# A gated-attention encoder layer on one core: first gates asked for together, the sixth product of the output moved, x on another queue, and a planner that costs accumulated weights differently

## The chip, the core and the metric

The kernel runs on one core of a Trainium2 chip. Time is device time in microseconds. The core has five engines that run side by side, each in the order of its own instructions: TensorE (PE; its weight loads are listed as PEld), VectorE (DVE), ScalarE (ACT), GpSimd (POOL) and SyncE (SP). SP, ACT and POOL also issue DMA transfers, which 16 DMA engines carry out. Matmul results land in PSUM banks.

## What is computed

One layer of a streaming encoder with 512 tokens of width 2048. The input is normalized and multiplied by one wide matrix. Its columns serve three token mixers of four heads each (q, k, v and a gate path per head), a forget gate, and three merge gates of width 2048. The mixers are A (softmax attention with a cumulative forget bias), B (chunked attention with a relative bias) and C (stick-breaking attention). Cut to what matters:

```python
hn = rmsnorm(x, norm_g)
proj = jnp.einsum('bsd,dc->bsc', hn, w_in)
gates = jax.nn.sigmoid(proj[..., QKVG_COLS + N_HEADS:] + b_gate).reshape(b, s, N_BRANCH, D_MODEL)
...
ys = jnp.stack([from_heads(ya), from_heads(yb), from_heads(yc)], axis=2)
ys = ys * jax.nn.silu(br[:, :, :, 3])
up = jnp.einsum('bsnw,nwd->bsnd', ys, w_up)
merged = jnp.sum(gates * up, axis=2)
return x + jnp.einsum('bsd,de->bse', merged, w_out)
```

## The kernel before

**Products in three parts.** All operands are float32. A weight tile arrives in a buffer named raw (there are eight), ACT rounds it to wh (line 366), and DVE subtracts to get the rest, wl (line 371). The activations are split in the same way into a high and a low part. A product is then three matmuls: high by wh, low by wh, high by wl. There are three wh buffers and two wl buffers, so ACT and DVE work two or three units ahead of PE.

**Units.** The work of PE is a list of units, each with one weight tile of 128 × 2 × 512 numbers (512 KB). Line 265 issues their matmuls into banks named acc. The list begins with the first head of C and one gate group as plain products (two blocks of x, kt, to a unit; the first two units hold one each). Then come eleven groups of one head and one gate group, then the up-projections, and then the output in two halves (`out_task(0)` and `out_task(1)`).

**Seven products in place of eight.** A head and a gate group, or half of the output, form a 2 × 2 block product that is made by Strassen's scheme in Winograd's form: seven products, numbered here, in the plain order 5, 1, 6, 7, 4, 2, 3, each of four units of 12 matmuls. Products 5 and 7 need a difference or sum of two weight blocks: SP fetches the one, and POOL adds the other into the same buffer with an accumulating DMA (`add_up`, line 281). Products 6 and 3 load nothing. Their weights are made by DVE, which adds the raw of product 1 to that of product 5 for the sixth (`sum_up`, line 574), and later that of product 2 for the third. So the raw buffers of product 5 are held until product 3 has been split.

**The output's first half.** Its operands are the merged blocks m, of which the last four pairs are ready only when the last up-projection is done; they are turned by PE (line 1285) and combined and split by `merged_a` and `merged_b`. Its unit order is written by hand: products 5, 1 and 6 on the first two quarters of the depth, then the same on the other two, then 7, 4, 2, 3. Product 6 has its banks in att (the attention's pool) there, because 5 and 1 hold the four banks of acc. The second half uses the plain order.

**The merge gates.** Each gate block goes through HBM (`gl`). `gates_of` fetches one (tile sg) and takes its sigmoid on ACT (line 1235). `up_units` makes, for each of the column groups g = 0, 2, 1, 3 and each mixer b, two units over four banks (tb = 0 to 3); when a bank is done, DVE multiplies it by its gate (line 1251) and so frees it. The fetches are attached to positions in the unit list, before the units that use them: at the third last unit for tb 0 and 1, at the second last for tb 2 and 3.

**The planner.** The order of the instructions on PE, ACT and DVE is written out by a planner in the kernel (`Flow`). Each piece of work is a generator that yields what it waits for, or an engine, a cost and perhaps a due time. The planner keeps a clock per engine and always takes the piece that can start first, and of those the one with the earliest due time. When a transfer lands is believed from a model: `landing` for plain ones and `add_up` for accumulating ones, both on one shared `line`. SP and POOL aren't among the three engines; the framework orders their transfers itself.

**The start.** A burst of 42 products of a small identity matrix (`WARM`, line 417) precedes the first real product. The constants come on ACT's queue, x and the weights on SP's. For the first two blocks of x, ACT makes the high part straight from x, with the norm's weight as scale, and DVE the low part (lines 434 and 437); for the later ones x is scaled first (line 445 or 448) and then split (lines 246 and 250).

Of the kernel before, what the change touches and what calls it, by code (L numbers as in the profile page):

```python
# [8 lines left out]
F32 = mybir.dt.float32  # L9
F32R = mybir.dt.float32r  # L10
BF16 = mybir.dt.bfloat16
AF = mybir.ActivationFunctionType
# [3 lines left out]
P = 128  # L16
S = 512
# [9 lines left out]
CH = 4  # L27
# [1 line left out]
HS = S // 2  # L29
EPS = 1e-6  # L30
NEG = -1e30
WARM = 42
SCALE = HD ** -0.5
LA = 2

A, B, C = 0, 1, 2
Q, K, V, G = 0, 1, 2, 3
PE, ACT, DVE = 0, 1, 2
# [116 lines left out]
def act_us(n, x=1):  # L155
    return x * (0.075 + 0.00095 * n)


def dve_us(n, x=1):
    return x * (0.1 + 0.00105 * n)  # L160
# [3 lines left out]
def hybrid_kernel(  # L164
# [12 lines left out]
    nc = tc.nc  # L177
    PS = bass.MemoryType.PSUM

    cp = ctx.enter_context(tc.tile_pool(name="cp", bufs=1))  # L180
    xp = ctx.enter_context(tc.tile_pool(name="xp", bufs=NX))
    wp = ctx.enter_context(tc.tile_pool(name="wp", bufs=3))
    tp = ctx.enter_context(tc.tile_pool(name="tp", bufs=NT))
# [7 lines left out]
    def nm(s):  # L191
        uid[0] += 1
        return f"{s}_{uid[0]}"

    flow = Flow()
# [4 lines left out]
    def t2(s, dt=F32):  # L200
        return tp.tile([P, S], dt, tag="t2", name=nm(s))
# [7 lines left out]
    def att():  # L209
        return pt.tile([P, S], F32, tag="att", name=nm("att"))  # L210

    def f(ap):
        return ap.bitcast(F32)
# [6 lines left out]
    def two(ap):  # L220

        return ap.rearrange("p (h s) -> p h s", h=2)
# [20 lines left out]
    def split(hi, lo, src, n, ev=None, due=(), hi_ev=None):  # L243

        yield (ACT, act_us(n), *due)
        nc.scalar.activation(hi, src, AF.Copy)  # L246
        if hi_ev is not None:
            set_(hi_ev)
        yield (DVE, dve_us(n), *due)
        nc.vector.tensor_sub(lo, src, f(hi))  # L250
        if ev is not None:
            set_(ev)
# [15 lines left out]
    line = [0.0, 0.0]  # L268
# [7 lines left out]
    def fetch(to, src, ready, kb):  # L276
        nc.sync.dma_start(to, src)
        return Event(landing(ready, kb))

    def add_up(to, src, ready, kb):  # L280
        nc.gpsimd.dma_start(to, src, accum_op=ALU.add)  # L281
        line[1] = max(line[1], ready + 1.0) + kb / 170.0
        return Event(line[1] + 2.5)

    def stored(slots, n, kb):

        slots.free += [landing(flow.fin, kb)] * n
# [1 line left out]

    nc.scalar.preload_act_table_set("natural_log_exp_and_others")  # L290
    small_in = cp.tile([P, consts.shape[1]], F32, name="small_in")
    nc.scalar.dma_start(small_in, consts)
    gn = small_in[:, 0:KT]
    gqk = small_in[:, KT:KT + 4]
    bfc = small_in[:, KT + 4:KT + 5]
    wf = small_in[:, KT + 5:].rearrange("p (k h) -> p k h", h=NH)

    epsc = cp.tile([P, 1], F32, name="epsc")
    nc.gpsimd.memset(epsc, EPS)
    nhepsc = cp.tile([P, 1], F32, name="nhepsc")  # L300
# [8 lines left out]
    identb = cp.tile([P, P], BF16, name="identb")  # L309
# [26 lines left out]
    units = []  # L336
    side = {}

    def at(u, g, slack=5.0):
        side.setdefault(u, []).append((g, slack))  # L340
# [20 lines left out]
    def prep(u):  # L361
        n = u.shape[0] * S
        u.hi = wp.tile([P] + u.shape, F32R, tag="wh", name=nm("wh"), bufs=LA + 1)
        yield u.there
        yield ACT, act_us(n)
        nc.scalar.activation(u.hi, u.raw, AF.Copy)  # L366
        set_(u.ready_hi)
        yield wls, 1
        u.lo = wp.tile([P] + u.shape, F32R, tag="wl", name=nm("wl"), bufs=LA)
        yield DVE, dve_us(n)  # L370
        nc.vector.tensor_sub(u.lo, u.raw, f(u.hi))  # L371
        set_(u.ready)
        u.split_done()
# [38 lines left out]
    xraw, x_in = [None] * KT, [Event() for _ in range(KT)]  # L412
    first_ps = att()
    atts.free.pop()
    nc.vector.memset(first_ps, 0.0)
    for _ in range(WARM):
        nc.tensor.matmul(first_ps[:, :P], identb, identb, start=True, stop=True)
    xps.free.clear()


# [5 lines left out]
    def prep_x(kt):  # L426

        due = (5.0 + 3.2 * kt,)
        yield x_in[kt]
        x = xraw[kt]  # L430
        if kt < 2:
            g = gn[:, kt:kt + 1]
            yield (ACT, act_us(S), *due)
            nc.scalar.activation(xs[kt].hi, two(x), AF.Copy, scale=g)
            set_(raw_hi[kt])
            yield (DVE, dve_us(S), *due)
            nc.vector.scalar_tensor_tensor(xs[kt].lo, two(x), g, f(xs[kt].hi), op0=ALU.mult, op1=ALU.subtract)
            set_(raw_ev[kt])
            yield (DVE, 0.5, due[0] + 5.0)
            nc.vector.tensor_scalar_mul(x, x, g)  # L440
            set_(scaled[kt])
            return
        if kt < 10:
            yield (DVE, 0.5, *due)
            nc.vector.tensor_scalar_mul(x, x, gn[:, kt:kt + 1])
        else:
            yield (ACT, 0.65, *due)
            nc.scalar.activation(x, x, AF.Copy, scale=gn[:, kt:kt + 1])
        set_(scaled[kt])
        yield from split(xs[kt].hi, xs[kt].lo, two(x), S, raw_ev[kt], due, raw_hi[kt])  # L450
# [127 lines left out]
    PLAIN = [(p, c) for p in (5, 1, 6, 7, 4, 2, 3) for c in range(CH)]  # L578
# [649 lines left out]
    def gates_of(n, g, tb):  # L1228
        yield last_head.event("hl", 2)
        yield t2s, 1  # L1230
        t = sig[n, g, tb] = t2("sg")
        yield fetch(t, gl[n, g, tb], flow.now, 256)
        yield last_head.event("g")
        yield ACT, act_us(S) + 0.1
        nc.scalar.activation(t, t, AF.Sigmoid)  # L1235
        set_(sig_ev[n, g, tb])
# [41 lines left out]
    def turned_m(g, i):  # L1278
        for tb in range(QB):
            yield merged_ev[NB - 1, g, tb]  # L1280
        yield atts, 1
        yield PE, 0.11 * QB
        ps = att()
        for tb in range(QB):
            nc.tensor.transpose(ps[:, blk(tb)], merged[g, tb][:, blk(i)], identf)  # L1285
        turns[g] = turns.get(g, 0) + 1
        if turns[g] == QB:
            give(t2s, QB)
        yield t2s, 1
        yield ACT, act_us(S)  # L1290
        m = t2("m")
        nc.scalar.activation(m, ps, AF.Copy)
        give(atts)
        k = 4 * g + i
        if k < UK:
            kept_m[k] = m
            spawn(merged_a(k, m), 4.0, flow.fin)
        else:
            spawn(merged_b(k - UK, m), 3.0, flow.fin)
# [48 lines left out]
    for g in (0, 2, 1, 3):  # L1348
        for b in range(NB):
            for tb in range(QB):  # L1350
                at(len(units) - 3 + tb // 2, lambda n=(C, B, A)[b], g=g, tb=tb: gates_of(n, g, tb))
            units.extend(up_units(g, b))
        for i in range(QB):
            at(len(units) - 1, lambda g=g, i=i: turned_m(g, i))
# [6 lines left out]
    def out_task(i):  # L1361
        where = dict(c11=(0, 0), c12=(2, 0), c21=(0, 1), c22=(2, 1))

        def place(name, tb):
            b, q = where[name]
            return b + tb, 2 * i + q

        def done(name, tb, c):
            yield ACT, 0.05
            nc.scalar.dma_start(out[place(name, tb)[0], place(name, tb)[1]], c)  # L1370
            stored(t2s, 1, 256)

        def rest(name, tb):
            return xn[place(name, tb)[0], place(name, tb)[1]]

        def src(m, half, c):
            return w_out[2 * i + m, CH * half + c]

        order, other = PLAIN, ()
        if i == 0:  # L1380
            order = [(p, c) for cs in ((0, 1), (2, 3)) for p in (5, 1, 6) for c in cs]
            order += PLAIN[3 * CH:]
            other = (6,)
        return Strassen(src, mops, done, order, other, rest).units

    for i in range(2):
        units.extend(out_task(i))


    def loads():  # L1390
        def x(kt):
            yield t2s, 1
            xraw[kt] = t2("x")
            x_in[kt].t = fetch(xraw[kt], xT[kt], 0.0, 256).t

        def n(i):
            n_in[i].t = fetch(xnat[i // 2][:, i % 2, :], xn[i // NQ, i % NQ], 0.0, 256).t

        order = [("x", 0), ("w", 0), ("x", 1), ("w", 1), ("x", 2), ("x", 3), ("w", 2)] + [("n", i) for i in range(4)]
        order += [("x", 4), ("x", 5), ("w", 3)] + [("n", i) for i in range(4, 8)]  # L1400
        order += [("x", 6), ("x", 7), ("w", 4)] + [("n", i) for i in range(8, 12)]
        order += [("x", 8), ("x", 9), ("w", 5)] + [("n", i) for i in range(12, 16)]
        for i in range(6, 9):
            order += [("x", 2 * i - 2), ("x", 2 * i - 1), ("w", i)]
        for kind, i in order:
            if kind == "x":
                yield from x(i)
            elif kind == "n":
                n(i)
            else:  # L1410
                yield from units[i].load()
        for u in units[9:]:
            yield from u.load()
# [12 lines left out]
                spawn(u.after(), 0.0, flow.fin)  # L1426

    line[0] = 0.8
    flow.fin = 5.0
    spawn(loads(), 0.0, 0.0)  # L1430
    for kt in range(KT):
        spawn(prep_x(kt), 5.0)
# [62 lines left out]
```

## Time and profile before

| | |
|---|---|
| median of 3 runs | 1318.59 us (1318.33 to 1319.23) |
| the profiled execution | 1318.87 us, of which span 1317.2 us |
| granted TensorE clock | 1.00 |
| PE, PEld, DVE, ACT, POOL busy | 99%, 82%, 78%, 57%, 7% of the span |
| DMA moved | 266.03 MB, mean 202 GB/s |
| accumulating transfers (POOL) | 88 of w_col, 16 of w_out, 512 KB each |

A row of the timeline gives start, duration, engine, line, operation and tiles, and in brackets how long the engine had been idle and what ended that. Rows next to each other may overlap, since a matmul's end is modelled and the next one starts before it. A row of waits gives the waiting engine and line, what ended the waits, their sum, their number and the longest. A row of the chain gives start, duration and what the time belongs to.

### The profile page before, as it was taken

What the parts mean: (1) busy time and instruction counts of PE and PEld (TensorE: products, weight loads), DVE (VectorE), ACT (ScalarE), POOL (GpSimd) and SP (SyncE); (2) the same over time, 40 slices, a digit from 0 to 9 for tenths busy, and PEclk for the clock granted to TensorE, in tenths of its full rate; (3) what the DMA queues carried; (4) which work ended last, traced back from release to release, by engine and by line L of the source; (5) the groups of instructions that cost most, each with busy time, mean ns of one, the idle gap of its engine ahead of it and who ended that gap; (6) DMA issues with size and microseconds to landing.
All of it is one profiled execution on the core that took longest, in us unless ns stands there. A gap on an engine that the chain in (4) does not pass through costs nothing.

```text
span 1317.2 us, 17191 instructions
## 1 busy us (share of the span) xinstructions
PE 1306.8 (99%) x6034; PEld 1078.7 (82%) x6034; DVE 1023.2 (78%) x1420; ACT 751.5 (57%) x1271; POOL 91.2 (7%) x115
## 2 busy tenths in 40 slices
PE   9999999999999999999999999999999999999998
PEld 7788888888888888888888888888887788878787
DVE  5877787887878777687776877778789668798667
ACT  7655464564557656566466654667568555454342
POOL 0000001110011100111011110110000000000110
PEclk9999999999999999999999999999999999999999
DMA  9755677866778757777577775777776656648883
GB/s 358 218 139 147 182 209 190 231 176 178 207 196 231 197 166 232 176 225 205 170 226 176 224 208 168 224 176 224 220 250 197 235 192 208 161 97 249 245 240 128
DMA packets 89063, 266.03 MB, mean 202 GB/s; under 512 B 11264, under 2 KB 11264, under 8 KB 88976
## 3 DMA queue, kind: packets, MB, share of 16 engines
q1 hardware_dynamic: 71552, 206.16, 46.5%
q0 software_dynamic: 14976, 54.53, 23.1%
q10 hardware_dynamic: 2448, 4.24, 0.8%
q8 instruction: 47, 0.77, 0.2%
q14 instruction: 40, 0.33, 0.1%
HBM read 245.19 MB, written 19.70 MB: 201 GB/s over the span
## 4 chain that ended last, share of the span: by engine, by line
PE 96%; DMA 2%; DVE 1%; ACT 1%; issue 0%; SPq 0%; ACTq 0%; POOLq 0%; DVEq 0%
PE acc L265 89%; DMA raw<-in_w_out 2%; PE att L801 1%; PE att L926 1%; PE att L260 1%; PE att L261 1%; PE att L262 1%; PE att L1016 1%; PE att L1015 1%; PE att L1285 1%; PE att L1014 1%; PE att L265 1%; ACT sg L1235 0%; DVE wl L371 0%; PE att L1118 0%; DMA x<-in_xT 0%
## 5 line engine op out<-in xcount | busy, mean ns | idle before, releaser
L371 DVE TENSOR_TENSOR wl<-raw,wh 128x1024 fp32r<-128x1024 f32 (+1 forms) x405 | 493.5, 1220 | 208.1 <-PE acc L265 116.1
L366 ACT ACTIVATE wh<-raw 128x1024 fp32r<-128x1024 f32 (+1 forms) x405 | 426.0, 1054 | 365.8 <-PE acc L265 276.3
L265 PE MATMUL acc<-wh,x 128*128 128x512 f32 x1664 | 429.8, 392 | 0.1
L265 PEld LDWEIGHTS acc<-wh,x 128*128 128x128 f32 x1664 | 308.7, 188 | 64.7 <-ACT t L246 0.9
L265 PE MATMUL acc<-wh,t 128*128 128x512 f32 x1056 | 272.6, 391 | 0.0
L265 PE MATMUL acc<-wl,x 128*128 128x512 f32 x832 | 229.8, 390 | 0.0
L265 PEld LDWEIGHTS acc<-wh,t 128*128 128x128 f32 x1056 | 196.7, 188 | 40.2
L265 PEld LDWEIGHTS acc<-wl,x 128*128 128x128 f32 x832 | 155.9, 188 | 33.1 <-DVE wl L371 0.4
L265 PE MATMUL acc<-wl,t 128*128 128x512 f32 x528 | 149.3, 390 | 0.0
L281 POOL DMA_DIRECT2D raw<-in_w_col x88 | 76.0, 864 | 877.5 <-ACT wh L366 195.3
L574 DVE TENSOR_TENSOR raw<-raw,raw 128x1024 f32<-128x1024 f32 x104 | 126.7, 1218 | 0.0
L265 PEld LDWEIGHTS acc<-wl,t 128*128 128x128 f32 x528 | 98.4, 188 | 19.6
L265 PE MATMUL acc<-wh,m 128*128 128x512 f32 x416 | 105.1, 390 | 1.9 <-ACT wh L366 1.9
L265 PE MATMUL acc<-wh,y 128*128 128x512 f32 x384 | 103.7, 391 | 1.3 <-DVE sg L1251 1.3
L265 PEld LDWEIGHTS acc<-wh,m 128*128 128x128 f32 x416 | 77.9, 188 | 18.8 <-ACT wh L366 2.7
L265 PEld LDWEIGHTS acc<-wh,y 128*128 128x128 f32 x384 | 71.7, 188 | 16.8 <-DVE sg L1251 2.2
L265 PE MATMUL acc<-wl,y 128*128 128x512 f32 x192 | 59.7, 391 | 0.0
L265 PE MATMUL acc<-wl,m 128*128 128x512 f32 x208 | 58.1, 390 | 0.1
L246 ACT ACTIVATE ah<-att 128x512 fp32r<-128x512 f32 (+3 forms) x48 | 21.0, 437 | 48.2 <-PE att L926 48.2
L265 PEld LDWEIGHTS acc<-wl,m 128*128 128x128 f32 x208 | 38.9, 188 | 8.5 <-DVE wl L371 0.5
L250 DVE TENSOR_TENSOR al<-att,ah 128x512 fp32r<-128x512 f32 (+3 forms) x48 | 23.5, 489 | 25.5 <-ACT ah L246 24.8
L265 PEld LDWEIGHTS acc<-wl,y 128*128 128x128 f32 x192 | 35.7, 188 | 7.2
(179 smaller groups left out, 1114.3 us busy)
## 6 DMA issues: line engine op xcount, KB each, us to landing
raw<-in_w_col SPq DMA_DIRECT2D x235, 512.0 KB, 4.6
raw<-in_w_col POOLq DMA_DIRECT2D x88, 512.0 KB, 7.9
raw<-in_w_out SPq DMA_DIRECT2D x40, 512.0 KB, 3.9
raw<-in_w_up SPq DMA_DIRECT2D x24, 512.0 KB, 3.6
sg<-gl SPq DMA_DIRECT2D x48, 256.0 KB, 4.6
raw<-in_w_out POOLq DMA_DIRECT2D x16, 512.0 KB, 6.2
gl<-u SPq DMA_DIRECT2D x22, 256.0 KB, 9.8
gl<-s SPq DMA_DIRECT2D x22, 256.0 KB, 5.2
```

The costliest lines, as they stand in the source:

```text
L246: nc.scalar.activation(hi, src, AF.Copy)
L250: nc.vector.tensor_sub(lo, src, f(hi))
L260: nc.tensor.matmul(ps, lh, rh, start=start, stop=False, skip_group_check=more)
L261: nc.tensor.matmul(ps, lh, rl, start=False, stop=False, skip_group_check=more)
L262: nc.tensor.matmul(ps, ll, rh, start=False, stop=stop, skip_group_check=more)
L265: nc.tensor.matmul(ps, w, x, start=start, stop=stop, skip_group_check=more)
L281: nc.gpsimd.dma_start(to, src, accum_op=ALU.add)
L366: nc.scalar.activation(u.hi, u.raw, AF.Copy)
L371: nc.vector.tensor_sub(u.lo, u.raw, f(u.hi))
L574: nc.vector.tensor_add(to.raw, to.raw, self.raw)
L801: nc.tensor.transpose(ps[:, blk(tb)], self.c[tb][:, blk(r)], identf)
L926: nc.tensor.transpose(ps[:, blk(i)], self.p[i][:, blk(j)], identf)
```

## The change

It has four parts.

1. Gates: the four first gate fetches (g = 0, b = 0) are attached to one position, the second last unit before the up-projections. All others stay.
2. Output, first half: its order becomes 5, 1 on the first two quarters, 5, 1 on the other two, and then the plain order from product 6 on. Product 6 takes its banks from acc.
3. Start: x's first block is fetched from ACT's queue and the constants from SP's. The warm-up has 36 products on a matrix of ones, which DVE fills, and writes another bank. DVE makes the first unit's wh. Four blocks of x instead of two take the path with the scale in ACT's pass, and the scaling that they need later is due at 24.
4. Planner: an accumulate takes `kb / 250` of the line, without waiting on it for the fetch before it, and lands 6.5 after the later of the line and that fetch; before, it took `kb / 170` from 1.0 after the fetch on and landed 2.5 after that. The believed start is 4.0 instead of 5.0, and x's first block is believed there at 3.6 and takes nothing of the line.

```diff
-WARM = 42
+WARM = 36
...
     def add_up(to, src, ready, kb):
         nc.gpsimd.dma_start(to, src, accum_op=ALU.add)
-        line[1] = max(line[1], ready + 1.0) + kb / 170.0
-        return Event(line[1] + 2.5)
+        line[1] += kb / 250.0
+        return Event(max(line[1], ready) + 6.5)
...
-    nc.scalar.dma_start(small_in, consts)
+    nc.sync.dma_start(small_in, consts)
+    x_first = tp.tile([P, S], F32, tag="t2", name=nm("x"))
+    nc.scalar.dma_start(x_first, xT[0])
...
+    oneb = cp.tile([P, P], BF16, name="oneb")
+    nc.vector.memset(oneb, 1.0)
...
-        yield ACT, act_us(n)
-        nc.scalar.activation(u.hi, u.raw, AF.Copy)
+        if u is units[0]:
+            yield DVE, dve_us(n)
+            nc.vector.tensor_copy(u.hi, u.raw)
+        else:
+            yield ACT, act_us(n)
+            nc.scalar.activation(u.hi, u.raw, AF.Copy)
...
+    early_ps = att()
     for _ in range(WARM):
-        nc.tensor.matmul(first_ps[:, :P], identb, identb, start=True, stop=True)
+        nc.tensor.matmul(early_ps[:, :P], oneb, oneb, start=True, stop=True)
...
-        if kt < 2:
+        if kt < 4:
...
+            if kt == 0:
+                yield units[0].ready_hi
             yield (DVE, dve_us(S), *due)
             nc.vector.scalar_tensor_tensor(xs[kt].lo, two(x), g, f(xs[kt].hi), op0=ALU.mult, op1=ALU.subtract)
             set_(raw_ev[kt])
-            yield (DVE, 0.5, due[0] + 5.0)
+            yield (DVE, 0.5, 24.0)
...
-                at(len(units) - 3 + tb // 2, lambda n=(C, B, A)[b], g=g, tb=tb: gates_of(n, g, tb))
+                at(len(units) - (3 - tb // 2 if g or b else 2), lambda n=(C, B, A)[b], g=g, tb=tb: gates_of(n, g, tb))
...
-            order = [(p, c) for cs in ((0, 1), (2, 3)) for p in (5, 1, 6) for c in cs]
-            order += PLAIN[3 * CH:]
-            other = (6,)
+            order = [(p, c) for cs in ((0, 1), (2, 3)) for p in (5, 1) for c in cs]
+            order += PLAIN[2 * CH:]
...
+            if kt == 0:
+                xraw[0], x_in[0].t = x_first, 3.6
+                return
...
-    flow.fin = 5.0
+    flow.fin = 4.0
```

## The prediction

> **What bounds the kernel now.** I read the page first, then PE's own waits, then the chain that ended last in order of time, and last the timeline at every place where PE waited.
>
> ```profile
> span 1317.2 us, 17191 instructions
> PE 1306.8 (99%) x6034; PEld 1078.7 (82%) x6034; DVE 1023.2 (78%) x1420; ACT 751.5 (57%) x1271; POOL 91.2 (7%) x115
> PE 96%; DMA 2%; DVE 1%; ACT 1%; issue 0%; SPq 0%; ACTq 0%; POOLq 0%; DVEq 0%
> ...
> PE att L417 <- DVE identb L310: 1.9, 1, 1.9
> PE acc L265 <- ACT wh L366: 1.9, 2, 1.4
> PE acc L265 <- DVE sg L1251: 1.3, 1, 1.3
> PE att L265 <- DVE wl L371: 1.1, 1, 1.1
> ...
> 670.26 22.72 PE acc L265 x100
> 1190.70 29.93 PE acc L265 x132
> ```
>
> TensorE bounds the kernel nearly everywhere: 96% of the chain. The change leaves out no product of the computation (only 6 of 42 warm-up products), so it can win only what PE loses by waiting. The ends of matmuls are modelled, so a short wait hides in the busy time; I measure by the beat instead. In the chain 132 products of 512 columns take 29.93 us, 0.2267 us each, and in the middle of a head 100 take 22.72 us, 0.2272 each. The heads run on the beat, with nothing to gain. Where a stretch takes longer than its number of products times 0.2267, the rest is lost. PE's waits name four places: the start, the first gates (DVE sg), one product in att (DVE wl), and a late pair behind ACT wh. I take them in the order of the diff.
>
> **Gates in order (line 1351).** These are timeline rows around the first merge gates.
>
> ```profile
> 1025.10 2.20 ACT L1235 ACTIVATE sg<-sg 128x512 f32<-128x512 f32 x4
> ...
> 1027.66 1.07 PE L265 MATMUL acc<-wh,y 128*128 128x512 f32 x4
> 1027.72 1.14 ACT L1235 ACTIVATE sg<-sg 128x512 f32<-128x512 f32 x2
> ...
> 1029.71 3.22 ACT L1235 ACTIVATE sg<-sg 128x512 f32<-128x512 f32 x6
> ...
> 1031.40 1.29 DVE L1251 TENSOR_TENSOR sg<-acc,sg 128x512 f32<-128x512 f32 x2 [1.12 <-ACT sg L1235]
> ...
> 1032.14 1.20 PE L265 MATMUL acc<-wh,y 128*128 128x512 f32 x4 [1.29 <-DVE sg L1251]
> ...
> 1033.64 1.09 PE L265 MATMUL acc<-wh,y 128*128 128x512 f32 x4
> ```
>
> DVE multiplies four finished banks by their gates and so frees them for the next branch's products. The third multiplication starts at 1031.40 and ends a wait for ACT. By then ACT had made 4, 2 and three of 6 sigmoids (1029.71 plus three of 0.54 is 1031.3): the third bank waited for the ninth gate, so the gates weren't made in the order in which they are used. From 1027.66 to 1033.64 PE issues 18 products (4, 2, 4, 2, 4, 2) in 5.98 us; on the beat 4.08. Lost: **1.9 us**. With all four first gates asked for at one place and in order they are the first four sigmoids, made by 1027.3. Three multiplications of 0.65 (1.29 for two) behind them fit before the third bank is asked for (1027.66 plus 12 products, 1030.4). What is late next is the second branch's first gate, wanted 30 products or 7 us after 1027.66. The edit adds no instruction; the two earlier fetches (256 KB each) are asked for one unit (12 products, 2.7 us) later, on SP. I take 1.9; bounds 0 (the ninth gate is only replaced by another late one) and 1.9.
>
> **The sixth product moved (lines 1380 to 1383).** The same view, 140 us later.
>
> ```profile
> 1167.50 1.22 DVE L574 TENSOR_TENSOR raw<-raw,raw 128x1024 f32<-128x1024 f32 x1
> 1168.83 2.01 ACT L366 ACTIVATE wh<-raw 128x1024 fp32r<-128x1024 f32 x2 [1.86 <-DVE raw L574]
> ...
> 1169.08 1.07 PE L265 MATMUL att<-wl,m 128*128 128x512 f32 x4
> ...
> 1171.91 1.22 DVE L371 TENSOR_TENSOR wl<-raw,wh 128x1024 fp32r<-128x1024 f32 x1
> ...
> 1173.18 1.20 PE L265 MATMUL att<-wl,m 128*128 128x512 f32 x4 [1.12 <-DVE wl L371]
> ...
> 1174.22 1.98 PE L265 MATMUL acc<-wh,m 128*128 128x512 f32 x8
> ```
>
> Now the sixth unit of the first output half belongs to product 6 (its bank is in att). Its weights are the sum of two others: DVE adds them at 1167.50, only then ACT rounds, only then DVE makes wl, and between these steps stand the splits of the last merged blocks. From 1169.08 to 1174.22 PE issues 16 products in 5.14 us, 3.63 on the beat. Lost: **1.5 us**. After the change this place holds product 5, whose weights come straight from memory; both sums (1.22 each) have four more units, 10.9 us, and product 6's merged operands too. The 28 units stay 28, and no load changes place, because product 6 loads nothing: 5, 5, 1, 1, 5, 5, 1, 1 is already the order of the loads, and they fill the eight raw buffers exactly. Product 6 now takes two banks of acc; those of 5 and 1 are copied out by ACT before. I take 1.5; bounds 0 and 1.5.
>
> **The start.** The first rows are the timeline, the last that of a view by stretches (PE, PEld, DVE, ACT, POOL busy; granted clock; DMA share; GB/s).
>
> ```profile
> 0.84 0.39 ACTq L292 DMA_DIRECT2D small_in<-in_consts  x1
> ...
> 1.93 4.31 PE L417 MATMUL att<-identb 128*128 128x128 bf16 x42 [1.93 <-DVE identb L310]
> ...
> 5.00 0.72 ACT L434 ACTIVATE x<-x,small_in 128x512 fp32r<-128x512 f32 x1 [2.90 <-DMA x<-in_xT]
> 5.62 0.61 ACT L366 ACTIVATE wh<-raw 128x512 fp32r<-128x512 f32 x1
> ...
> 6.29 2.11 PE L265 MATMUL acc<-wh,x 128*128 128x512 f32 x8
> ...
> 21.63 1.06 ACT L366 ACTIVATE wh<-raw 128x1024 fp32r<-128x1024 f32 x1 [0.22 <-DMA raw<-in_w_col]
> ...
> 22.75 3.50 PEld L265 LDWEIGHTS acc<-wh,x 128*128 128x128 f32 x16 [0.16 <-ACT wh L366]
> 22.85 3.82 PE L265 MATMUL acc<-wh,x 128*128 128x512 f32 x16
> ...
> 6.00:33.00 27.00, 26.94 (x122) 21.94 (x120) 18.15 (x30) 22.46 (x54) 0.00 (x0) 1.00 1.04 393
> ```
>
> The first product waits for x on ACT (0.72) and then for the first wh on ACT (0.61). The change puts that wh on DVE beside it, sends x from ACT's queue at about 0.8 while the small constants go to SP, and ends the warm-up sooner. So the first product can start 0.6 to 1.0 us earlier, at about 5.3. But it isn't kept. From 6 to 33 us the DMA engines are full (share 1.04, 393 GB/s); the fifth unit's weights land at 21.63, ACT rounds them by 22.69, PE reads them at 22.75 and starts at 22.85, just when its earlier work is through. The bytes ahead of these weights are the same in either queue, so PE comes a microsecond earlier to the fifth unit and waits there. I take **0.1** (22.85 to 22.75); bounds: a loss of 0.4 (one more issue of 0.39 ahead of the first weights on SP, if it delays every later load) and a gain of 1.0. The scaling of two more blocks moves from in front of ACT's pass to behind DVE's, work that PE covers, for nothing.
>
> **The planner's accumulates.** The new cost lines add no instruction; they move the believed landing of accumulated weights and of all loads behind them, and so the order written out for PE, ACT and DVE in every head. Two rows bear on it, one of ACT's waits and one of the chain.
>
> ```profile
> ACT wh L366 <- DMA raw<-in_w_col: 26.6, 12, 3.8
> ...
> 1222.27 9.44 DMA raw<-in_w_out
> ...
> 1232.26 11.08 DMA raw<-in_w_out
> ```
>
> ACT already stands before late weights 12 times, 2.2 us each time, and PE doesn't feel it in the heads. I take 0: the heads are on the beat before and have cover. Above, the bound is what a third of that wait would cost in each of the 11 later heads, 0.7 × 11 = 8 us; below, what PE loses at the fourth place.
>
> ```profile
> 1214.00:1218.00 4.00, 4.00 (x20) 3.30 (x19) 4.00 (x6) 1.97 (x2) 0.00 (x0) 1.00 0.28 79
> 1226.00:1242.00 16.00, 15.57 (x69) 12.58 (x68) 7.51 (x7) 3.50 (x4) 1.72 (x2) 1.00 1.05 292
> ...
> 1238.60 1.07 PE L265 MATMUL acc<-wl,m 128*128 128x512 f32 x4
> ...
> 1246.38 1.08 PE L265 MATMUL acc<-wh,m 128*128 128x512 f32 x4
> ```
>
> There, at the second output half, 22 products take 7.78 us instead of 4.99: **2.8 us** lost. The chain shows why: a fetch of 9.44 us and an accumulate of 11.08 behind it. The DMA engines idle at 1214 to 1218 (share 0.28; all raw buffers taken, DVE busy 4.00 of 4) and are full from 1226 to 1242 (1.05). The gate is DVE's freeing of buffers, which the change doesn't touch, so I leave the 2.8 in.
>
> **Sum.** 1.9 + 1.5 + 0.1 = 3.5 us off the profiled execution's 1318.87 (span 1317.2 and 1.67 around it): 1315.4. The median of the runs is 0.28 below that execution, so **1315.1**.
>
> **The rivals.**
> - *The tail takes it back.* If the late pair's landing is set by the full DMA engines from 1226 on and not by the buffers, PE only comes earlier to the same landing, and the 3.4 us won ahead of it come back as a longer wait there. For it: share 1.05. Against it: the idle stretch just before, which moves with PE. Time: 1318.5 if all comes back, about 1317 if half. Chance 0.25.
> - *The new plan stalls the heads* (the slower side). An accumulated weight believed to land too early has its wh put too early in ACT's queue; the attention's copies queue behind it, and the transposes and attention products, in order on PE, wait for those copies. Place: ACT in front of a wh, once per head. Price: 0.7 us in each of 11 heads, 8 us, so 1322.8. It decides from 0.3 us per head (3.5 / 11); the result is slower by over 0.2% from 0.55. For it: the 26.6 us of such waits now. Against it: PE shows none of them. Chance 0.20.
> - *The plan also mends the tail.* If DVE's sums for the last product come earlier, 2.8 more go: 1312.3. Chance 0.10.
> - *The shorter warm-up leaves PE slow.* The warm-up's rate rises within it:
>
> ```profile
> 5.00:5.50 0.50, 0.50 (x7) 1.00 0.89 315
> 5.50:6.00 0.50, 0.50 (x10) 1.00 1.03 389
> ```
>
>  Seven starts in half a microsecond become ten, some 3.6 us after the first warm-up product, although the granted clock is shown as 1.00 in both. At the slow rate 128 columns take 4.31 / 42 = 0.103 us, so 512 take 0.41 and not 0.227. Thirty-six take 3.7 us, and the burst ends near the rise. If the rise came 3.7 us later still, nine real products would each be 0.18 slower, 1.7 us, less the 1.0 by which they start sooner: 0.7 worse, 1315.8. Chance 0.05. [...]
>
> **How the numbers follow.** The forecast has 0.40. About 0.2%, 2.6 us, can be told from no change here: faster means below 1315.95, slower above 1321.2. Faster: 0.38 of the forecast, 0.02 of the warm-up case, 0.10 of the mended tail: 0.50. Same: 0.25 of the tail rival and 0.05 from the edges: 0.30. Slower: 0.20. The range runs from 1311.0 (mended tail and a start that keeps the whole 1.0 us) to 1323.0 (the stalled heads at their price); the other end of the heads' case lies outside.
>
> **What would show it.** Right: sigmoids in order and no PE wait for DVE sg near 1030; no wait for DVE wl near 1173 and product 6 in acc only; first product near 5.3 but the fifth unit still near 22.7; the wait at the late pair unchanged. Wrong: PE waits inside the heads, periods that differ from before by more than a few tenths, a fifth unit well ahead of 22.7, or a late pair that waits longer by what was won before it.

## The result and the profile after

| | before | changed |
|---|---|---|
| median of the runs shown with the change, us | 1318.76 (1318.26 to 1319.23, 6 runs) | 1313.85 (1313.41 to 1316.47, 6 runs) |
| time of the profiled execution, us | 1318.87 | 1313.92 |
| its span, us | 1317.2 | 1312.2 |

The ratio is 0.9966, with a 95% interval from 0.9956 to 0.9977. The gain of 4.9 us is real and a little larger than the 3.5 us of the forecast; the time lies in the range that was given (1311.0 to 1323.0).

The page of the changed kernel opens like this (span, busy time of the engines, shares of the chain that ended last):

```profile
span 1312.2 us, 17142 instructions
PE 1305.7 (100%) x6028; PEld 1079.2 (82%) x6028; DVE 1026.5 (78%) x1422; ACT 756.4 (58%) x1270; POOL 91.3 (7%) x115
PE 95%; DMA 3%; ACT 1%; SPq 0%; DVE 0%; issue 0%; ACTq 0%; POOLq 0%
```

PE's busy time fell by only 1.1 us while the span fell by 5.0. The modelled ends of the matmuls hide short waits in the busy time, so the list of PE's waits says more. It has two entries left, the warm-up's own start and one wait at the late pair (us in total, times, longest):

```profile
PE acc L265 <- ACT wh L374: 1.3, 1, 1.3
PE att L426 <- DVE oneb L301: 1.1, 1, 1.1
```

The waits for DVE sg and for DVE wl are gone. The timeline around the first merge gates shows why:

```profile
1024.80 2.20 ACT L1246 ACTIVATE sg<-sg 128x512 f32<-128x512 f32 x4
...
1025.46 0.69 DVE L1262 TENSOR_TENSOR sg<-acc,sg 128x512 f32<-128x512 f32 x1 [1.65 <-ACT sg L1246]
```

ACT's first four sigmoids are now made in one run, and by the instruction order of the changed kernel these four are the gates that DVE multiplies first. In the kernel before, the same four gates were the first, second, ninth and tenth sigmoid; the ninth and tenth were those of token blocks 0 and 1. DVE starts on a gate 0.66 us after its sigmoid began, and PE has no wait there.

The chain of the changed kernel from the last merge turn to the end (start, us, what):

```profile
1154.16 1.75 PE att L1296 x16
1155.90 59.35 PE acc L265 x262
1215.25 1.14 DVE wl L379
1216.61 1.24 DVE wl L379
1217.87 9.78 DMA raw<-in_w_out
1227.71 0.49 issue
1228.20 10.12 DMA raw<-in_w_out
1238.43 1.07 ACT wh L374
1239.52 1.24 DVE wl L379
1240.80 67.42 PE acc L265 x296
```

After the last turn PE issues 262 products without a stop: 262 × 0.2267 = 59.4 us. The sixth unit lies in this piece and costs nothing any more. The late pair is still there: a fetch, an accumulate of 10.12 us behind it, then ACT, then PE.

Where the 5.0 us of the span came from, by positions in the two chains. The rows of the kernel before are these:

```profile
39.53 1.83 PE att L1118 x16
...
911.05 5.02 PE acc L265 x22
...
1053.77 1.75 PE att L1285 x16
...
1156.83 1.75 PE att L1285 x16
...
1245.81 67.40 PE acc L265 x296
```

and these, with the two rows of 1154.16 and 1240.80 above, those of the changed one:

```profile
39.29 1.83 PE att L1129 x16
...
911.01 5.02 PE acc L265 x22
...
1051.10 1.75 PE att L1296 x16
```

| stretch | before | changed | difference |
|---|---|---|---|
| start to the forget logits (L1118, now L1129) | 39.53 | 39.29 | −0.24 |
| heads, to 911 | 871.52 | 871.72 | +0.20 |
| last head and first gates, to the first turn | 142.72 | 140.09 | −2.63 |
| the four turns | 103.06 | 103.06 | 0.00 |
| last turn to the last 296 products | 88.98 | 86.64 | −2.34 |
| the last 296 products | 67.40 | 67.42 | +0.02 |

Two places won, one lost a little, and the start, where most lines of the change stand, gave a quarter of a microsecond. That is less than two executions of one kernel differ by there: a second trace of the changed kernel, further below, has the forget logits at 38.79 and not at 39.29.

### The profile page after: what moved, and what is told of

Same layout as the page of the kernel before. It is cut to its first block, busy times and chain, and to the rows that moved or that the text cites. A ratio compares the mean times of both kernels' runs of the same rounds, so it can differ in the third digit from the quotient of the medians.

```text
span 1312.2 us, 17142 instructions
## 1 busy us (share of the span) xinstructions
PE 1305.7 (100%) x6028; PEld 1079.2 (82%) x6028; DVE 1026.5 (78%) x1422; ACT 756.4 (58%) x1270; POOL 91.3 (7%) x115
## 4 chain that ended last, share of the span: by engine, by line
PE 95%; DMA 3%; ACT 1%; SPq 0%; DVE 0%; issue 0%; ACTq 0%; POOLq 0%
PE acc L265 89%; DMA raw<-in_w_out 2%; PE att L812 1%; PE att L937 1%; DMA x<-in_xT 1%; PE att L1027 1%; DMA raw<-in_w_col 1%; PE att L1026 1%; PE att L261 1%; PE att L262 1%; PE att L260 1%; PE att L1025 1%; PE att L1296 1%; SPq L277 0%; PE att L1129 0%; DVE wl L379 0%
## 5 line engine op out<-in xcount | busy, mean ns | idle before, releaser
L265 PE MATMUL acc<-wh,x 128*128 128x512 f32 x1664 | 434.4, 393 | 0.1
L585 DVE TENSOR_TENSOR raw<-raw,raw 128x1024 f32<-128x1024 f32 x104 | 126.5, 1218 | 0.0
L265 PE MATMUL acc<-wh,m 128*128 128x512 f32 x448 | 113.1, 389 | 1.3 <-ACT wh L374 1.3
L265 PEld LDWEIGHTS acc<-wh,m 128*128 128x128 f32 x448 | 84.0, 188 | 19.2 <-ACT wh L374 1.7
L265 PE MATMUL acc<-wl,m 128*128 128x512 f32 x224 | 62.6, 390 | 0.1
L265 PE MATMUL acc<-wl,y 128*128 128x512 f32 x192 | 59.4, 391 | 0.0
L265 PEld LDWEIGHTS acc<-wl,m 128*128 128x128 f32 x224 | 41.8, 188 | 9.2 <-DVE wl L379 0.7
L246 ACT ACTIVATE ah<-att 128x512 fp32r<-128x512 f32 (+3 forms) x48 | 20.9, 436 | 30.2 <-PE att L937 30.2
L1262 DVE TENSOR_TENSOR sg<-acc,sg 128x512 f32<-128x512 f32 x48 | 32.8, 689 | 5.0 <-PE acc L265 2.6
```

Source lines behind the costliest of these rows:

```text
L265: nc.tensor.matmul(ps, w, x, start=start, stop=stop, skip_group_check=more)
L585: nc.vector.tensor_add(to.raw, to.raw, self.raw)
L1262: nc.vector.tensor_mul(t, ps[tb], t)
```

## The experiments

The first four put one part of the change alone into the kernel before. They ran on one chip and share its runs of the kernel before: 1318.9 us (1317.84 to 1320.73, 33 runs).

### The gates alone

```diff
-                at(len(units) - 3 + tb // 2, lambda ...
+                at(len(units) - (3 - tb // 2 if g or b else 2), lambda ...
```

> The kernel before with only the gates edit. Theory A (each part is worth what PE lost at its own place): PE's wait for DVE sg near 1032 is gone, the stretch from 994 to the first turn of the merged blocks is 1.9 us shorter, everything else stands, so 1316.9 against 1318.8. Theory B (the gates edit is worth the whole 2.7 us that the stretch lost in the changed kernel): 1316.1. Theory C (most of it comes from the planner's new costs): under 1 us.

Measured: 1316.95 us (1316.14 to 1317.38), ratio 0.9982 [0.9973, 0.9991], 1.95 less. PE's wait for DVE sg is gone, and the stretch from the last head to the first turn is 1.90 shorter (1051.21 − 910.39 = 140.82 against 142.72). The wait of 1.9 us was the price of the order, and nothing took it back later.

### The sixth product alone

```diff
-            order = [(p, c) for cs in ((0, 1), (2, 3)) for p in (5, 1, 6) for c in cs]
-            order += PLAIN[3 * CH:]
-            other = (6,)
+            order = [(p, c) for cs in ((0, 1), (2, 3)) for p in (5, 1) for c in cs]
+            order += PLAIN[2 * CH:]
```

> The kernel before with only the order of the output's first half. Theory A: the wait for DVE wl near 1173 goes, 1.5 us, and the late pair of the second half still loses 2.8: 1317.3. Theory B (the new order also brings the second half's loads earlier, which would explain the 0.9 us that the changed kernel won there): 2.4 us, 1316.4. Rival from the prediction (the tail takes it back): 1318.8, with a late pair that loses over 4 us.

Measured: 1317.24 us (1316.42 to 1317.97), ratio 0.9987 [0.9978, 0.9996], 1.66 less. In its chain 315 products run from the last turn on without a stop:

```profile
1156.78 1.75 PE att L1285 x16
1158.53 71.52 PE acc L265 x315
...
1241.72 1.06 ACT wh L366
...
1244.09 67.41 PE acc L265 x296
```

PE came to the late pair 1.5 us sooner and still got past it 1.67 sooner (87.31 against 88.98 after the last turn). The landing behind it, ACT's row, came at 84.94 after the last turn and not at 86.61 (1243.44 − 1156.83). So the landing moves with PE, and the tail doesn't take the gain back. That fits buffers which are freed by work that PE's progress drives.

### The start alone

The edit is everything of the change in the start: x first on ACT's queue, the constants on SP's, the first wh on DVE, the warm-up of 36 products from a tile of ones, the moved due times, and the planner's believed start.

> The kernel before with only the start's edits (x on ACT's queue, constants on SP's, 36 warm-up products on ones, first wh on DVE, four blocks on the short path, believed start 4.0). Theory A (the DMA engines are full, so the earlier first product is waited away by the sixth or seventh unit): first product at 5.1 instead of 6.3, the logits of the forget gate (16 products of 4 rows) at 39.2 instead of 39.5, total 0.25 less: 1318.5. Rival: the gain of 1.2 us is kept in this kernel and was lost in the changed one by its plan: 1317.6.

Measured: 1318.45 us (1317.92 to 1321.82), ratio 1.0003 [0.9994, 1.0011]: nothing that can be told from no change. The forget logits stand at 39.37. The timeline of the changed kernel, which has the same start, shows what became of the earlier first product:

```profile
1.13 4.02 PE L426 MATMUL att<-oneb 128*128 128x128 bf16 x36 [1.13 <-DVE oneb L301]
...
3.86 0.72 ACT L443 ACTIVATE x<-x,small_in 128x512 fp32r<-128x512 f32 x1 [1.77 <-DMA x<-in_xT]
...
4.50 0.43 DVE L371 CAST wh<-raw 128x512 fp32r<-128x512 f32 x1 [0.66 <-DMA raw<-in_w_col]
```

Its chain a little later, up to the forget logits:

```profile
26.44 1.06 ACT wh L374
27.50 2.45 ACT xn L487 x8
...
33.13 0.62 ACT x L459
33.77 0.64 ACT x L246
34.45 4.83 PE acc L265 x20
```

PE's own timeline, and two stretches (PE, PEld, DVE, ACT, POOL busy with their counts, where a product that reaches over an edge counts on both sides; granted clock; DMA share; GB/s):

```profile
5.07 2.67 PE L265 MATMUL acc<-wh,x 128*128 128x512 f32 x8
```

```profile
5.50:6.00 0.50, 0.50 (x2) 0.38 (x2) 0.50 (x2) 0.50 (x1) 0.00 (x0) 1.00 0.96 315
6.50:7.00 0.50, 0.50 (x4) 0.42 (x3) 0.50 (x2) 0.28 (x1) 0.00 (x0) 1.00 1.27 397
```

The first product starts at 5.07 and not at 6.29, 1.22 us sooner. But the first eight take 2.67 us, where eight on the beat take 1.98 in such a row (and the first eight of the kernel before took 2.11): two products lie in half a microsecond at first and four from 6.5 on. The slow ones cost 0.56 more than before. Most of the rest goes at the sixth and seventh unit. The sixth unit's weights land at 26.33, ACT rounds them from 26.44 on, and PE loses 0.16 there against the beat. In the seventh unit PE issues four products at 33.18 and the next ones at 34.45, 0.36 late. It waits for the high part of a block of x, which ACT makes (L246) behind its sums for the norm (xn, L487), a rounding of weights and a scaling (L459). From 26.44 to 34.41 the chain runs over ACT alone. The DMA engines are full in either kernel (share 1.04 from 6 to 33 us), and the chain leads back to them through the weights that land at 26.33; whether the bytes or ACT's queue hold PE, this run doesn't separate.

### The planner's costs alone

```diff
-        line[1] = max(line[1], ready + 1.0) + kb / 170.0
-        return Event(line[1] + 2.5)
+        line[1] += kb / 250.0
+        return Event(max(line[1], ready) + 6.5)
```

> The kernel before with only the two cost lines of the accumulating transfers. Theory A: nothing at the start and at the two repaired places; the heads lose some 0.3 us in all and the tail wins some 0.9: 1318.2. Rival 1 (the plan is what mended part of the gates' stretch): 0.8 more, 1317.4. Rival 2 (the plan costs the heads): over 1319.4.

Measured: 1318.03 us (1317.06 to 1319.25), ratio 0.9992 [0.9983, 1.0001]: 0.87 less, with an interval that just reaches no change. By the chain it costs 0.20 in the heads (911.30 − 118.69 = 792.61 from the first to the last head, 792.41 before) and wins 1.15 at the late pair:

```profile
1156.85 1.75 PE att L1285 x16
...
1242.31 1.06 ACT wh L366
...
1244.68 67.40 PE acc L265 x296
```

The landing stands 85.46 after the last turn, 1.15 sooner than before. The four medians add up to 1.95 + 1.66 + 0.45 + 0.87 = 4.9, which is what all four parts together won. That doesn't show that the parts are independent: the 0.45 can't be told from nothing, and the next run shows that the plan is worth more beside the others.

### The changed kernel with the old costs

The edit is that of the last experiment, backwards, in the changed kernel. This run and the next three share one chip and its runs of the kernel before: 1318.81 us (1317.93 to 1320.18, 15 runs).

> The changed kernel with the old two cost lines back. Theory A (the plan is worth 0.9 to 1.2 us by itself, nearly all of it at the late pair of the second half, and costs the heads 0.2): 1314.9 against 1313.9 of the changed kernel, heads 0.2 shorter, late pair losing 2.8 instead of 1.9. Rival (with gates and sixth product repaired the plan no longer matters): 1313.9.

Measured: 1316.57 us (1314.71 to 1318.05), ratio 0.9981 [0.9973, 0.999]. That is 2.7 us more than the changed kernel, well above what was expected of the plan. The chain and the timeline (PE alone) of this kernel show the surplus behind the late pair:

```profile
1154.69 1.75 PE att L1296 x16
...
1240.08 1.06 ACT wh L374
...
1242.44 69.01 PE acc L265 x296
```

```profile
1241.18 1.20 PE L265 MATMUL acc<-wh,m 128*128 128x512 f32 x4 [2.39 <-ACT wh L374]
1242.44 0.99 PE L265 MATMUL acc<-wl,m 128*128 128x512 f32 x2
1243.24 1.91 PE L265 MATMUL acc<-wh,m 128*128 128x512 f32 x4
```

```profile
1238.00:1242.00 4.00, 1.61 (x8) 1.00 (x6) 0.83 (x1) 1.92 (x3) 0.00 (x0) 1.00 0.65 251
1242.00:1246.00 4.00, 3.94 (x11) 2.80 (x10) 2.66 (x3) 1.63 (x3) 0.00 (x0) 0.59 0.12 13
```

PE waits 2.39 us. In the four microseconds behind the wait the granted clock is 0.59, and 11 products lie in it where 18 lie on the beat. The last 296 products take 69.01 us and not 67.42: 1.6 us on top of the wait. The wait itself is 1.1 longer than in the changed kernel (the landing stands 85.39 after the last turn, against 84.27 there).

### Later loads for the norm

In the changed kernel the 16 blocks of xn, which are fetched four at a time behind the weights of the third to sixth unit, are spread behind those of the fourth to ninth.

```diff
-        order = [...("x", 3), ("w", 2)] + [("n", i) for i in range(4)]
...
+        n_at = {3: (0, 2), 4: (2, 4), 5: (4, 7), 6: (7, 10), 7: (10, 13), 8: (13, 16)}
+        for i in range(3, 9):
+            order += [("x", 2 * i - 2), ("x", 2 * i - 1), ("w", i)] + [("n", j) for j in range(*n_at[i])]
```

> The changed kernel with the 16 loads for the norm (4 MB) spread behind the fourth to ninth unit's own loads, the same bytes in all. Theory A (full DMA engines take the start's 1.2 us back): PE stays on the beat from its first product at 5.1, the logits of the forget gate start near 38.4 instead of 39.3, total 0.9 less than the changed kernel: 1313.0. Rival (ACT, busy 9.9 of 10 us there, holds PE at the seventh unit anyway): logits at 39.2, 1313.8. Third possibility: the norm is ready too late for the first head, and PE waits near 49: over 1314.5.

Measured: 1313.08 us (1312.67 to 1315.93), ratio 0.9961 [0.9947, 0.9974], 0.8 less than the changed kernel. From 11.38 to the forget logits PE now runs in one piece:

```profile
10.27 1.07 ACT wh L374
11.38 27.49 PE acc L265 x120
38.88 1.83 PE att L1129 x16
```

120 products take 27.49 us, 0.229 each: nothing is lost at the sixth and seventh unit any more, but 0.3 us behind a weight that lands at 10.25. The logits start at 38.88, 0.41 sooner than in the changed kernel's first trace and not 0.9 as hoped; its second trace has them at 38.79, so by the logits of single traces nothing is shown. The better comparison is between the next two kernels, which ran on one chip and differ in this edit alone: 1312.15 and 1311.43 us, and the slowest run of the second (1311.63) is faster than the fastest of the first (1311.93). So the spread loads are worth some 0.7 us. With the bytes, the edit also moves ACT's sums over them to later times, so it doesn't show which of the two had held PE.

### The first product's plain weights ahead

In the changed kernel the second output half takes product 1, whose weights come straight from memory, ahead of product 5, whose weights are accumulated.

```diff
+        else:
+            order = [(p, c) for p in (1, 5, 6, 7, 4, 2, 3) for c in range(CH)]
```

> The changed kernel with product 1 (plain loads) before product 5 (accumulated loads) in the output's second half. Theory A (PE waits there for the landing of product 5's accumulates, and nothing else is late): the wait for wh near 1239 goes, 1.9 us, 1312.0. Rival (the full DMA engines only make other weights late): the wait moves to product 1 or 7, 1313.8.

Measured: 1312.15 us (1311.93 to 1313.04), ratio 0.9951 [0.9938, 0.9963], 1.7 less than the changed kernel. PE goes from the last turn to the end in one piece:

```profile
1156.94 150.39 PE acc L265 x663
```

663 products in 150.39 us are 0.2268 each. The same work takes 1308.22 − 1155.90 = 152.3 us in the changed kernel: the late pair cost 1.9 there.

### Both

The last two edits together, in the changed kernel.

> The changed kernel with the norm's loads spread and product 1 before 5. If both theories hold, the sum: 0.9 + 1.9 less than the changed kernel, 1311.1. If only the tail's holds, 1312.0; if only the start's, 1313.0.

Measured: 1311.43 us (1311.11 to 1311.63), ratio 0.9944 [0.9931, 0.9956]. This is the fastest of all, 2.4 us below the changed kernel, and its five runs lie within 0.5 us. Against the later loads alone, on the same chip, the order of the products is worth 1.65. The only PE wait for data that its trace lists is 0.5 us ahead of the first products.

### Two runs once more

What the plan is worth beside the other edits came from runs that weren't made side by side, and the fall of the clock from a single trace there. So the changed kernel and the one with the old costs ran again, on one chip (kernel before: 1319.05 us, 1318.28 to 1320.2, 15 runs).

> The changed kernel once more, on one chip beside the next run, since the plan's worth (2.7 us beside the other edits, 0.9 alone) came from runs of separate calls. Both theories: 1313.4 to 1314.2 as a median, the x296 piece of the chain 67.4 us long. A change of the median by more than 0.7 us would say that the difference between calls is as large as what was compared.

Measured: 1313.39 us (1313.0 to 1315.49, 5 runs), ratio 0.9959 [0.9947, 0.9972]; the last 296 products take 67.39.

> The changed kernel with the old costs of add_up, once more, on the same chip as the run before it. Theory A (the plan is worth about 1.1 us by the wait itself, and the rest is TensorE's clock, which falls behind the longer wait in some executions only): runs spread from about 1314.9 to 1318.1, median 1.0 to 2.8 us above the changed kernel; the profiled execution waits 2.3 to 2.5 us at the late pair, and if the granted clock is under 0.9 in some stretch behind the wait the x296 piece is 1 us or more longer than 67.4, if it is 1.00 throughout it is 67.4. Theory B (the 1.6 us behind the wait was an accident of the one profiled execution, and the plan is worth its wait alone): all runs within 0.7 us of a median 0.9 to 1.3 us above the changed kernel.

Measured: 1317.11 us (1314.85 to 1318.16, 11 runs), ratio 0.9982 [0.9973, 0.9991]. The difference is 3.7 us, above both theories. The spread is that of the first: of the 11 runs the three with a mean clock of 1.000 have a median of 1315.17, which is 1.8 above the changed kernel, and the six with 0.998 one of 1317.16. The wait of the profiled execution, 1.92, is shorter than the 2.3 to 2.5 that the first theory gave. The profiled execution waits and then slows down again (chain, timeline of PE, stretches):

```profile
1155.43 1.75 PE att L1296 x16
1241.46 69.92 PE acc L265 x300
```

```profile
1241.46 1.73 PE L265 MATMUL acc<-wh,m 128*128 128x512 f32 x4 [1.92 <-ACT wh L374]
```

```profile
1242.00:1246.00 4.00, 4.00 (x12) 3.02 (x12) 2.94 (x3) 1.90 (x3) 0.00 (x0) 0.59 0.02 6
```

300 products take 69.92 and not 68.0 us on the beat: the clock was no accident of one trace. The chains of the two kernels now give the plan's worth piece by piece, nearly the same from both pairs (the first pair of traces, then the second): heads +0.21 and +0.21, last head and first gates −0.72 and −0.69, late landing −1.1 and −1.1 (83.87 after the last turn against 84.92), and from the landing to the end −1.6 and −1.3. That is 3.2 and 2.8 us. Between the two executions of the second pair lie 4.1 us, and the rest of these is the start: this profiled execution had its logits at 40.07, against 38.79 in the run beside it, with the same lines of code in the start.

## Why the prediction was right, and where it was not

**What bounds the kernel.** Right. The beat of 0.2267 us told where time was lost, and the gain came for the most part at the places that it had named; 0.7 of it came in the last head, where no wait was listed. The heads moved by 0.2 us in 872, the turns not at all.

**The gates.** Right in mechanism and size: 1.9 forecast, 1.95 alone, and 1.90 of the stretch.

**The sixth product.** Right: 1.5 forecast, 1.66 alone, and the sixth unit is on the beat. The step that no load changes place fits as well, since the late pair didn't get later.

**The start.** The size was right (0.1 forecast; −0.24 in the trace, nothing measurable alone), but the way to it was not, so the size is partly luck. The first product came 1.22 us sooner, beyond the 0.6 to 1.0 of the forecast. The fifth unit wasn't where PE met the loads again: ACT rounded its weights at 20.06 this time and not at 21.63, and it started at 22.09, well ahead of 22.7, which the prediction had named as a sign of being wrong. Of the 1.2 us some 0.56 had gone before that, to slow products. That is the loss that the rival "the shorter warm-up leaves PE slow" had named, at a third of its 1.7 us, and by itself it decided nothing; no run changed the burst alone, so its cause wasn't shown. The sixth and seventh unit took most of the rest back, the larger part by a wait for ACT's pass over x and not for weights. The cause that was given, full DMA engines, is at the head of that chain; that it decides and not ACT's queue was not shown.

**The planner's accumulates.** This is the step that failed. The term was taken at 0, and the 2.8 us of the late pair were left in with the reason that the gate there is DVE's freeing of buffers, "which the change doesn't touch". But DVE's order is written by the planner, and in it stand the sums that make product 3's weights and free the buffers of product 2 (L574, now L585). After the last turn these four sums start at 56.5, 58.2, 61.6 and 64.5 us in the changed kernel with the old costs, and at 54.1, 58.7, 59.9 and 64.4 with the new ones: the first and the third come sooner by 2.3 and 1.7. All four traces with the new costs and product 5 ahead have the two middle sums in one run, and none of the six with the old costs has. The last accumulate is issued 74.0 after the last turn and not 75.1. So the term was −0.9 alone, and the late pair, which was to stay at 2.8, fell to 1.9 in the changed kernel. Beside the other edits it was about −3: a part in the last head and the first gates that hadn't been thought of (0.7), the landing (1.1), and the clock behind the wait (1.6 and 1.3). That the sums are what moves the landing is argued from the order of these rows; no run moved the sums alone.

**The rivals.** *The tail takes it back* fell for the changed kernel, where the landing came 2.34 sooner after the last turn and the pair cost 1.9 and not 2.8. With the old costs it would have held in half: the other three parts together then gave 2.2 us (1316.57 against 1318.81), not the 4.1 that they gave one by one, because the pair then cost 0.3 more than in the kernel before and the clock fell behind it, for 1.6. Its place and its size, about 1317, were right; its cause, a landing set by full DMA engines, was for the most part not, since of the 1.5 us by which PE came sooner the landing had followed 1.2 even there. *The plan stalls the heads* was right in sign and wrong in size: 0.2 us over all heads, not 0.7 in each. *The plan also mends the tail* came true in part, 0.9 of 2.8; the two runs with product 1 ahead show that the other 1.9 were there to be had by an order.

**The sum.** 4.9 measured against 3.5 forecast; the planner's term makes up 0.9 of the 1.4 between them when measured alone. The rest (0.35 at the start, 0.16 at the sixth product, 0.05 at the gates) is within what the runs of one kernel differ by. The lower end of the range doesn't quite follow from its terms: 1318.59 − 1.9 − 1.5 − 1.0 − 2.8 is 1311.4, not 1311.0; nothing hangs on it. That the sum came so near is partly luck: the three terms that it did contain add up only because the term that it had left at nothing keeps the late pair's wait short.

## What to carry to other kernels

Count products against the beat to find what PE loses, because busy time can hide short waits (here it fell by 1.1 us where the span fell by 5.0); then look whether a free choice of order (which gate first, which product first) lets a late operand be wanted later (1.95 us for the gates, 1.66 for the sixth product). Where summed weights are late, as in this kernel's output, put a product whose weights come straight from memory ahead of them (1.7 us). A first product that came 1.22 us earlier was worth next to nothing here (1318.45 us against 1318.9) until the loads for the norm behind it, and with them ACT's work on them, were moved as well (some 0.7 us).

## What the runs showed of the hardware

- A wait of TensorE of 2.39 us, and in another execution one of 1.92, were followed by four microseconds at a granted clock of 0.59. On top of the wait 1.6 us went there in the first (69.01 against 67.42 for the last 296 products) and 1.3 in the second (71.06 against 69.77 from the landing to the end). Behind a wait of 1.6 us (the start alone) the clock was 0.67 from 1246 to 1250 and the last 296 products took 68.98; behind one of 1.55 us (the sixth product alone) they took 67.41. So of two waits of almost one length one was followed by slower products and one was not; what decides it was not found.
- A lower mean clock comes in some executions only, and in the kernel before as well: of its 33 runs beside the first four experiments, six have a mean clock of 0.998 and a median of 1320.39 us, 26 have 1.000 and 1318.71. Of the ten runs with product 1 ahead, whose profiled executions have no wait there, none is below 0.999. Where the clock fell in the runs that have no trace isn't shown.
- At the start the granted clock is shown as 1.00 while products come at about half rate. In the kernel before, the 42 warm-up products of 128 columns take 4.31 us, 0.103 each, where a quarter of the beat of 512 columns is 0.057. From 5.5 us on, 3.6 after the first of them, ten start in half a microsecond and not seven. In the changed kernel the 36 take 4.02 us, 0.112 each; its first products start at 5.07, 5.63, 6.06 and 6.42, and from there on come every 0.23 us, 5.3 after the first warm-up product.
- The same code of the start put the forget logits at 39.53, 38.87, 39.09 and 39.57 (kernel before, gates alone, sixth alone, plan alone), and the new start, with the loads for the norm where they were, at 39.29, 38.79, 39.37, 39.33, 40.07 and 40.32. A difference of half a microsecond in the first 40 us says nothing from one trace.
